# Output projection of a hybrid decoder block: where its weight buffers lie, in which order its transfers are queued, and how its norm sums are made

## Chip, cores and metric

The kernel is one program on one NeuronCore of a Trainium2 chip. The metric is the device time of one execution in microseconds (us). Engine names are those of the profile: PE is TensorE's matmul row, PEld its weight loads, DVE VectorE, ACT ScalarE, POOL GpSimd, SP SyncE. SP, ACT and POOL also issue transfers (DMAs).

## The reference

One block for 512 tokens of width 2048, in float32, with one batch and one layer:

```python
h = _rmsnorm(x, norm1_g) * (1.0 + sc1) + sh1
p = h @ w_in                                    # 2048 x 4384
y_rwkv = _rwkv7_mixer(p[..., :N_RWKV_COLS], ...)  # 16 heads of 64, delta-rule state
y_pool = _pool_mixer(p[..., N_RWKV_COLS:], ...)   # causal means over 2, 4, 8, 16 tokens
mix = jnp.concatenate([y_rwkv, y_pool], axis=-1) @ w_out   # 2048 x 2048
x = x + gt1 * mix
h = _rmsnorm(x, norm2_g) * (1.0 + sc2) + sh2
x = x + gt2 * _conv_ffn(h, w_up, conv_w, conv_b, w_down)   # 2048 x 11264, 5632 x 2048
return _rmsnorm(x, norm_f_g)
```

The shifts, scales and gates (sh, sc, gt) come from `silu(c) @ w_ada + b_ada`. `_rmsnorm` needs, for each token, the sum of squares over all 2048 features.

## The kernel before, in words

**Layout.** Features lie on the 128 partitions, tokens on the free axis, so x is 16 tiles of 128x512. Every float32 operand of the large products is split in two F32R parts, a high part (a cast by ACT) and a low part (the rest, by DVE), and a product is three matmuls: high by high, high by low, low by high (`mm3`, lines 136 to 138). A matmul's stationary operand is a 128x128 piece of a weight tile, its moving operand an activation tile of 256 or 512 columns.

**Stages.** First the modulation rows and the first product tiles. Then the mixer, with the input projection interleaved (`projection`, line 646: 27 tiles of 48 matmuls, 512 columns wide) in an order that a planner writes out by hand. Then the output projection, the subject here. Then the up projection with the conv, then the down projection. From the output projection on, the work is a list of steps which `pipeline` (line 1257) emits: for step i its matmuls, then the load of step i + 4 (LA = 4), the split of step i + 2, then the `after` functions of step i.

**The output projection** has four kinds of steps:

- Early blocks (`out_block`, 7 of them, 12 matmuls 512 wide) still run beside the mixer's end.
- `late_blocks`: 9 steps of 12 matmuls, 512 wide. Their after functions also make sums and differences of activation halves (`operands0`), which the next group needs.
- `out_group`: 4 rounds of 7 steps p1 to p7, each of 24 matmuls 256 wide, which is a Strassen-like scheme for half of the rows and columns. Steps p3 and p6 need a *sum* of two weight blocks. It is made by a plain load into a `wide` tile (line 1488, SP) and a second load by POOL that adds to it (line 1489, `accum_op=ALU.add`). Steps p1, p2 and p7 end in `stage_pair` (line 1432): ACT scales the result into a staging tile and POOL adds it into x by an accumulating DMA (line 1437). From round 1 on, p2 and p4 also call `out_done` (line 1527), which squares a finished x tile for the norm and stores it (line 1529, POOL).
- `out_halves`: 16 steps for the first token half (`lo`), 16 for the second (`hi`), 12 matmuls 256 wide each. Each `lo` step loads 256 KB of weights four steps before its matmuls.

After them `first_steps` begins the up projection (24 matmuls 256 wide a step).

**Weight buffers.** A split weight lies in one of two places. `wp` tiles `whi` and `wlo` (four of each) come from the pool at the right end of the memory; `wtile` (names `ow`, later `uw`) are three-part tiles in pool `ea`, whose parts are used from byte offset 64 (`off=16` floats) or 0. In the program as laid out, `whi` and `wlo` begin at byte addresses that are 0 mod 128, and a `wtile` begins at 0 mod 128, so its parts with `off=16` are at 64 mod 128. The moving operands are at 0 mod 128. The up and down projections use `wtile`s at offset 64 for 256 columns and at 0 for 512. In the output projection the ring of `split2` goes `wtile`, `wtile`, `wp`, `wp`; the late blocks and most halves are in `wp`.

**Order of issue.** Within an engine's queue the framework's scheduler orders instructions by its own estimate of when they are ready, unless `tc.issue_after` pins one behind another.

**Norm.** `norm_rows` sums the squares over partitions with four 1-column matmuls (line 185), takes ACT's Sqrt (line 190), a reciprocal on DVE (191), scales an identity by it (194), and `norm_bcast` spreads it with a float32 matmul (line 198). This is done for each token half, in `out_halves` and in `first_steps`, and again at the kernel's end.

Of the kernel before, what the change touches and what calls it, by code (L numbers as in the profile page):

```python
# [9 lines left out]
F32 = mybir.dt.float32  # L10
F32R = mybir.dt.float32r
# [57 lines left out]
def block_kernel(ctx, tc, a, out, stop=None, dbg=None):  # L69
# [50 lines left out]
    def load_weights(src, eng=nc.sync):  # L120
        raw = wp.tile([P, WC], F32, tag="wraw", name="wraw", bufs=4)
        eng.dma_start(raw, src)
        return raw
# [1097 lines left out]
    def wide(name):  # L1221

        return rb.tile([P, 4, HT], F32, tag="wide", name=name, bufs=3)
# [8 lines left out]
    def x2(f, sl=slice(0, T)):  # L1232
        return x2q[f // 4][:, f % 4, sl]
# [15 lines left out]
    nsplit, lo_of, hi_of, g_of = [0], [None], [None], [None]  # L1249

    class Step:

# [42 lines left out]
    def residual(f, pss, gate, acc, lo, hi, fresh):  # L1295
# [48 lines left out]
    for t, i0 in ((mixa, 4), (mixb, 8)):  # L1344
        for i in range(4):
            nc.sync.dma_start(t[:, i, :], mixd[MIX_ORDER[i0 + i]])
    x2q += [None] * 4

    def load_x2(q):
        x2q[q] = quad(q, "x2")  # L1350
        nc.sync.dma_start(x2q[q], a["xT"][:, 4 * q : 4 * q + 4, :])

# [5 lines left out]
    M += last_mix  # L1358
    for q in range(3):
        load_x2(q)  # L1360

    ngate = ea.tile([P, 3 * NF], F32, tag="ncw", name="ngate")
    V.tensor_scalar(ngate[:, 0:KT], mod[:, 32 : 32 + KT], -1.0, None, op0=ALU.mult)

# [21 lines left out]

    def osplit(raw, w=None, i=0):
        if w is None:
            hi, lo = (wp.tile([P, WC], F32R, tag=t, name=t, bufs=4) for t in ("whi", "wlo"))
        else:  # L1390
            hi, lo = (w[:, 16 + o + i * WC : 16 + o + i * WC + WC] for o in (0, 2 * QW))
        hi_of[0] = S.copy(hi, raw)
        lo_of[0] = V.tensor_tensor(lo, raw, hi.bitcast(F32), op=ALU.subtract)
        return hi, lo
# [3 lines left out]

    nring = [0]

    def split2(src):
        i = nring[0] % 4
        nring[0] += 1
        if i > 1:
            return [osplit(src[:, j * WC : j * WC + WC]) for j in range(2)]
        w = wtile(i)
        hi, lo = w[:, 16 : 16 + 2 * WC], w[:, 2 * QW + 16 : 2 * QW + 16 + 2 * WC]
        hi_of[0] = S.copy(hi, src)
        lo_of[0] = V.tensor_tensor(lo, src, hi.bitcast(F32), op=ALU.subtract)
        return [(hi[:, j * WC : j * WC + WC], lo[:, j * WC : j * WC + WC]) for j in range(2)]  # L1410
# [17 lines left out]
    def add_pair(f, hs, ps, sign=1):  # L1428
        for j in range(2):
            add_x2(f + j, hs, ps[:, j * HT : (j + 1) * HT], sign)  # L1430

    def stage_pair(f, hs, ps, sign=1):
        t = wp.tile([P, WC], F32, tag="wraw", name="stage", bufs=4)
        for j in range(2):
            g = mod[:, 32 + f + j : 33 + f + j] if sign > 0 else ngate[:, f + j : f + j + 1]
            S.activation(t[:, j * HT : (j + 1) * HT], ps[:, j * HT : (j + 1) * HT], AF.Copy, scale=g)
        G.dma_start(x2q[f // 4][:, f % 4 : f % 4 + 2, hs], t[:, :].rearrange("p (f t) -> p f t", f=2), accum_op=ALU.add)

    def raw_step(f, k0, mm, after, **kw):
        d = {}  # L1440

        def load():
            d["w"] = load_weights(a["wout"][f, :, k0 * P : k0 * P + WC])

        return Step(None, mm, after, load, split=kw.pop("split", None) or (lambda: osplit(d["w"])), **kw), d

    def late_blocks():
        out_, prep = [], operands0()
        for f, k0 in [(f, 12) for f in (4, 5, 6, 7, 0, 1, 2)] + [(3, 0), (3, 12)]:
            def mm(wh, wl, f=f, k0=k0):  # L1450
                if k0 == 0:
                    pss[f] = bank()
                block(pss[f], wh, wl, k0, slice(0, T), k0 == 0, k0 > 0, (f, k0) == (3, 12))
            done = [lambda f=f: add_x2(f, slice(0, T), pss[f])] if k0 else []
            out_.append(raw_step(f, k0, mm, [lambda: next(prep, None)] + done, hold=(f, k0) == (3, 12))[0])
        return out_

    o4 = []

    def out_group():  # L1460
# [8 lines left out]
        def buf(i):  # L1469
            while len(o4) <= i // 2:  # L1470
                o4.append(ea.tile([P, 4 * QW], F32, tag=f"t4{len(o4)}", name="ow4"))
            return o4[i // 2][:, (W1, W2)[i % 2]]

# [5 lines left out]
        for h in range(4):  # L1479
            f, d = 2 * h, {}  # L1480

            def plain(i, r, g):
                return lambda: nc.sync.dma_start(two(buf(i)), src(r, g))

            def both_(name, r1, g1, r2, g2, d=d):
                def load():
                    d[name] = wide(name).rearrange("p a b -> p (a b)")
                    nc.sync.dma_start(two(d[name]), src(r1, g1))
                    G.dma_start(two(d[name]), src(r2, g2), accum_op=ALU.add)
                return load  # L1490
# [32 lines left out]
        for h in range(4):  # L1523
            seq += out_[h][:5] + firsts[h + 1 : h + 2] + out_[h][5:]
        return seq

    def out_done(f):
        sumsq(acc, x2(f), 0, T, f == 0, o4[1][:, 2 * QW + f % 2 * T : 2 * QW + f % 2 * T + T])
        G.dma_start(x2d[f], x2(f))

    def half_done(f, hs, ps):
        add_x2(f, hs, ps)
        sumsq(acc, x2(f, hs), hs.start, hs.stop, False)
        G.dma_start(x2d[f][:, hs], x2(f, hs))

    first = {}

    def out_halves():
        kept, raws = {}, {}
# [12 lines left out]

        def raw(f, e):
            raws[f, e] = load_weights(a["wout"][f, :, 12 * e * P : 12 * e * P + WC])
# [19 lines left out]
        for j, (f, e) in enumerate(again):  # L1574
            hi[j].split = lambda f=f, e=e: kept[f, e]
        for j, n in zip((0, 1, 2, 3, 6, 7, 8, 9), range(8)):
            hi[j].load = lambda n=n: raw(*order[n])
        for j, i in ((1, 0), (3, 1)):
            hi[j].after[:0] = [lambda i=i, e=e: in_ea(8 + i, e, i) for e in range(2)]
        for n in range(4, 8):  # L1580
            hi[n + 1].after[:0] = [lambda n=n: in_wp(*order[n])]
        steps = first_half()
        hi[1].after.append(lambda: first.update(dg=norm_rows(acc[:, H0])))
        hi[3].after.append(lambda: first.update(rstd=norm_bcast(first["dg"])))
        for j in (4, 5, 6, 7, 9, 10, 11, 12):
            hi[j].after.append(lambda: next(steps, None))
# [86 lines left out]
    def first_steps():  # L1673
# [3 lines left out]
        for n in range(NB):  # L1677
            d = {}

            def load(sl, n=n):  # L1680
                if not rows:
                    rows.extend(ea.tile([P, 4 * QW], F32, tag=f"t4{i}", name="wrow") for i in range(2))
                nc.sync.dma_start(rows[n % 2][:, sl], a["wup"][2 * n, :, sl])

# [27 lines left out]
    halves, ups = out_halves(), first_steps()  # L1712
# [4 lines left out]
    pipeline(late_blocks() + out_group() + halves + ups)  # L1717
    for _ in steps:
# [208 lines left out]
    yd = [tc.dram_tile([P, T], F32, name=f"yd{f}") for f in range(KT)]  # L1927

    def queue(*args, **kw):
        with tc.issue_after(g_of[0].ins) if g_of[0] else nullcontext():  # L1930
            g_of[0] = G.dma_start(*args, **kw)

# [373 lines left out]
```

## Time and profile before

| | us |
|---|---|
| median of 3 runs | 2169.04 |
| lowest and highest of them | 2135.17, 2174.9 |
| profiled execution, its own time | 2138.61 |
| its span, first to last instruction | 2136.6 |

| engine | busy us | share of the span |
|---|---|---|
| PE | 2097.3 | 98% |
| PEld | 1874.0 | 88% |
| DVE | 1703.0 | 80% |
| ACT | 1055.4 | 49% |
| POOL | 262.0 | 12% |

A matmul's row in the profile gives the time from its start to its modelled end. Matmuls are pipelined, so that is longer than the distance from one start to the next; the distance is had from a stretch of the timeline divided by the matmuls in it.

### The profile page before, as it was taken

How to read it: one execution, taken by the hardware profiler on the slowest of the kernel's cores; microseconds unless marked ns; L12 is line 12 of the kernel's file. 1: busy time of each engine (PE TensorE's matmuls, PEld its weight loads, DVE VectorE, ACT ScalarE, POOL GpSimd, SP SyncE). 2: the span in 40 equal slices, each digit the busy share in tenths (PEclk: the TensorE clock that was granted, in tenths of full speed). 3: DMA queues.
4: the chain of work that ended last, by engine and by line, in shares of the span. 5: the costliest groups of instructions: out<-in, count | busy, mean ns of one | idle time of the engine just before them, and what ended most of it. 6: DMA issues, size and time to landing. Idle time of an engine off the chain costs nothing.

```text
span 2136.6 us, 44762 instructions
## 1 busy us (share of the span) xinstructions
PE 2097.3 (98%) x18216; PEld 1874.0 (88%) x18216; DVE 1703.0 (80%) x2649; ACT 1055.4 (49%) x1520; POOL 262.0 (12%) x400
## 2 busy tenths in 40 slices
PE   7999999999989999999999999999999999999997
PEld 3567777777767999999999999999999889998897
DVE  7988898989857867988888888877878658767775
ACT  4354444434434547655555555555556544453353
POOL 0002122211210321110011001000000000021100
PEclk9999999999999999999999999999999999999999
DMA  9966666656537975988988888877777645488865
GB/s 394 406 227 198 199 195 178 191 174 177 166 106 253 246 216 166 323 246 250 257 252 242 248 260 248 227 211 209 207 206 215 217 143 138 135 268 319 313 209 177
DMA packets 175792, 481.37 MB, mean 225 GB/s; under 512 B 21521, under 2 KB 32737, under 8 KB 166753
## 3 DMA queue, kind: packets, MB, share of 16 engines
q1 hardware_dynamic: 120914, 353.17, 47.9%
q0 software_dynamic: 33456, 87.59, 20.1%
q10 hardware_dynamic: 21216, 37.76, 5.8%
q8 instruction: 143, 2.34, 0.4%
q14 instruction: 63, 0.52, 0.1%
HBM read 438.05 MB, written 37.23 MB: 222 GB/s over the span
## 4 chain that ended last, share of the span: by engine, by line
PE 86%; issue 5%; DMA 3%; DVE 3%; ACT 1%; POOL 1%; POOLq 0%; DVEq 0%; ACTq 0%
PE b L138 21%; PE b L136 21%; PE b L137 21%; PE mm L646 10%; PE pf L427 4%; PE pb L1048 1%; DVE war L765 1%; PE pa L712 1%; DMA wa<-ada 1%; DMA wraw<-win 0%; PE pf L136 0%; PE pf L138 0%; PE pf L137 0%; POOL x L888 0%; PE pb L1088 0%
## 5 line engine op out<-in xcount | busy, mean ns | idle before, releaser
L138 PE MATMUL b<-t,uw 128*128 128x256 f32 x1408 | 388.6, 276 | 0.0
L136 PE MATMUL b<-t,uw 128*128 128x256 f32 x1408 | 388.6, 276 | 0.0
L137 PE MATMUL b<-t,uw 128*128 128x256 f32 x1408 | 388.6, 276 | 0.0
L136 PE MATMUL b<-y,uw 128*128 128x256 f32 x1056 | 292.0, 277 | 0.0
L137 PE MATMUL b<-y,uw 128*128 128x256 f32 x1056 | 291.6, 276 | 0.0
L646 PE MATMUL mm<-ahl,whi 128*128 128x512 f32 x864 | 289.6, 409 | 2.1 <-DVE rk L549 1.4
L138 PE MATMUL b<-y,uw 128*128 128x256 f32 x1056 | 291.5, 276 | 0.0
L138 PEld LDWEIGHTS b<-t,uw 128*128 128x128 f32 x1408 | 264.3, 188 | 0.0
L137 PEld LDWEIGHTS b<-t,uw 128*128 128x128 f32 x1408 | 264.3, 188 | 0.0
L136 PEld LDWEIGHTS b<-t,uw 128*128 128x128 f32 x1408 | 264.2, 188 | 0.0
L1619 DVE TENSOR_TENSOR uw<-r,uw 128x1024 fp32r<-128x1024 f32 x164 | 200.6, 1223 | 79.0 <-ACT uw L1618 78.7
L1619 DVE TENSOR_TENSOR uw<-wquart,uw 128x1024 fp32r<-128x1024 f32 x148 | 181.1, 1223 | 54.6 <-ACT uw L1618 54.5
L1618 ACT CAST uw<-r 128x1024 fp32r<-128x1024 f32 x164 | 172.8, 1053 | 73.0 <-PE b L138 73.0
L1619 DVE TENSOR_TENSOR uw<-wd,uw 128x1024 fp32r<-128x1024 f32 (+1 forms) x112 | 124.2, 1109 | 100.5 <-ACT uw L1618 100.5
L136 PE MATMUL b<-act,uw 128*128 128x256 f32 (+1 forms) x608 | 200.6, 330 | 0.0
L137 PE MATMUL b<-act,uw 128*128 128x256 f32 (+1 forms) x608 | 200.4, 330 | 0.0
L138 PE MATMUL b<-act,uw 128*128 128x256 f32 (+1 forms) x608 | 200.3, 330 | 0.0
L136 PEld LDWEIGHTS b<-y,uw 128*128 128x128 f32 x1056 | 198.3, 188 | 0.1
L137 PEld LDWEIGHTS b<-y,uw 128*128 128x128 f32 x1056 | 198.2, 188 | 0.0
L138 PEld LDWEIGHTS b<-y,uw 128*128 128x128 f32 x1056 | 198.1, 188 | 0.0
L646 PEld LDWEIGHTS mm<-ahl,whi 128*128 128x128 f32 x864 | 158.2, 188 | 43.2 <-issue 12.2
L1618 ACT CAST uw<-wquart 128x1024 fp32r<-128x1024 f32 x148 | 155.8, 1053 | 80.7 <-PE b L138 65.5
(406 smaller groups left out, 4812.4 us busy)
## 6 DMA issues: line engine op xcount, KB each, us to landing
wquart<-wup SPq DMA_DIRECT2D x176, 512.0 KB, 6.0
wa<-ada SPq DMA_DIRECT2D x48, 1024.0 KB, 9.5
war<-ada SPq DMA_DIRECT2D x192, 256.0 KB, 3.8
wd<-wdn SPq DMA_DIRECT2D x64, 512.0 KB, 4.6
wraw<-win ACTq DMA_DIRECT2D x118, 256.0 KB, 4.1
wquart<-wup POOLq DMA_DIRECT2D x44, 512.0 KB, 6.7
r<-wup SPq DMA_DIRECT2D x44, 512.0 KB, 4.6
r<-wup POOLq DMA_DIRECT2D x44, 512.0 KB, 8.1
```

The source lines that it names most:

```text
L136: muls = [lambda: PE.matmul(ps, wh, xh, start=start, stop=False, skip_group_check=more), lambda: PE.matmul(ps, wh, xl, start=False, stop=F ...
L137: lambda: PE.matmul(ps, wh, xl, start=False, stop=False, skip_group_check=more),
L138: lambda: PE.matmul(ps, wl, xh, start=False, stop=stop, skip_group_check=more)]
L427: PE.matmul(pf[n % 2 * 4 + ii], w[:, sl], full[k], start=k == 0, stop=k == KT - 1)
L646: PE.matmul(ps, w[:, sl], x, start=first, stop=k == KT - 1 and i == 2)
L712: PE.matmul(ps, pw[:, i, d * P : (d + 1) * P], zs[i], start=i == 0, stop=i == 1)
L765: V.scalar_tensor_tensor(wa, wa, 1.0, cqs[kq], op0=ALU.mult, op1=ALU.mult, accum_out=modq[:, kq, j : j + 1])
L1048: PE.matmul(pt[HS[e], h, c * 2 * L : (c + 1) * 2 * L], nt[HS[e], s, :], rw[HS[e], s, :, :], start=True, stop=True)
L1618: hi_of[0] = S.copy(hi, src)
L1619: lo_of[0] = V.tensor_tensor(lo, src, hi.bitcast(F32), op=ALU.subtract)
```

## The change

- 64 bytes of padding (`edge`) are put at the front of the `tables` and of the `wts` pool. `whi` and `wlo` move by 64 bytes to 64 mod 128; activations stay at 0 mod 128. This holds for all stages that use `wp`, the mixer's input projection too.
- The late blocks (512 wide) are split into `wtile`s at offset 0. The ring of `split2` begins with `wp`.
- All of POOL's transfers in the group and the halves go through `queue`, and SP's through `loadq`: each is pinned behind the one emitted before it. Splits are pinned in the same way (`parts`).
- The plain load of a p3 or p6 sum is issued one step earlier (`begin`); the accumulating load stays four steps ahead.
- The staging tile of `stage_pair` leaves the ring of four `wraw` tiles and uses two halves of a `t41` buffer. `out_done` squares into a PSUM bank in place of a buffer.
- Halves load their weights eight steps ahead, into four `wraw` tiles and four pieces of `t40`.
- x tiles are loaded in another order and partly later.
- The two norms of this stage use `norm_parts` and `norm_sum`: the sum of squares is split in two F32R parts, two 256-wide matmuls with a matrix of ones add over partitions and spread at once, and ACT's Ln and Exp make the inverse root. The norm at the kernel's end is unchanged.

```diff
+    tp.tile([P, 16], F32, tag="edge", name="edge")
+    wp.tile([P, 16], F32, tag="edge", name="edge", bufs=1)
...
+    def queue(*args, **kw):
+        with tc.issue_after(g_of[0].ins) if g_of[0] else nullcontext():
+            g_of[0] = G.dma_start(*args, **kw)
+
+    def loadq(*args):
+        with tc.issue_after(p_of[0].ins) if p_of[0] else nullcontext():
+            p_of[0] = nc.sync.dma_start(*args)
...
+    def norm_parts(acc):
+        t = rb.tile([P, 4, HT], F32R, tag="wide", name="sums", bufs=3)
+        S.copy(t[:, 0, :], acc)
+        V.tensor_tensor(t[:, 1, :], acc, t[:, 0, :].bitcast(F32), op=ALU.subtract)
+        return t
+
+    def norm_sum(t):
+        psb = bank()[:, 0:HT]
+        for i in range(2):
+            PE.matmul(psb, onesr, t[:, i, :], start=i == 0, stop=i == 1)
+        S.activation(psb, psb, AF.Ln, bias=eps[:, 0:1], scale=1.0 / D)
+        S.activation(psb, psb, AF.Exp, scale=-0.5)
+        return psb
...
-    for q in range(3):
+    for q in (1, 0):
         load_x2(q)
...
+    def parts(hi, lo, raw):
+        with tc.issue_after(hi_of[0].ins) if hi_of[0] else nullcontext():
+            hi_of[0] = S.copy(hi, raw)
+        with tc.issue_after(lo_of[0].ins) if lo_of[0] else nullcontext():
+            lo_of[0] = V.tensor_tensor(lo, raw, hi.bitcast(F32), op=ALU.subtract)
...
-    nring = [0]
+    nring = [2]
...
     def stage_pair(f, hs, ps, sign=1):
-        t = wp.tile([P, WC], F32, tag="wraw", name="stage", bufs=4)
+        t = buf(3)[:, nstage[0] % 2 * WC : nstage[0] % 2 * WC + WC]
+        nstage[0] += 1
...
-        G.dma_start(x2q[f // 4][...], ..., accum_op=ALU.add)
+        queue(x2q[f // 4][...], ..., accum_op=ALU.add)
...
+        def late_split(i, raw):
+            if i % 2 == 0:
+                w[i] = wtile(i // 2 % 2)
+            return osplit(raw, w[i - i % 2], i % 2, 0)
...
+        out_[2].after.append(lambda: load_x2(2))
...
             def both_(name, r1, g1, r2, g2, d=d):
                 def load():
+                    queue(two(d[name]), src(r2, g2), accum_op=ALU.add)
+
+                def begin():
                     d[name] = wide(name).rearrange("p a b -> p (a b)")
-                    nc.sync.dma_start(two(d[name]), src(r1, g1))
-                    G.dma_start(two(d[name]), src(r2, g2), accum_op=ALU.add)
+                    loadq(two(d[name]), src(r1, g1))
+                load.begin = begin
                 return load
...
+        for st, nxt in zip([begun] + seq, seq):
+            if nxt.load and hasattr(nxt.load, "begin"):
+                st.load = lambda a=nxt.load.begin, b=st.load: (a(), b() if b else None)
...
     def out_done(f):
-        sumsq(acc, x2(f), 0, T, f == 0, o4[1][:, 2 * QW + f % 2 * T : 2 * QW + f % 2 * T + T])
-        G.dma_start(x2d[f], x2(f))
+        sumsq(acc, x2(f), 0, T, f == 0, bank() if f else None)
+        queue(x2d[f], x2(f))
...
+        def raw(f, e, slot=0):
+            if slot > 3:
+                raws[f, e] = o4[0][:, (slot - 4) * WC : (slot - 3) * WC]
...
         for b, (f, e) in enumerate(order):
-            lo[b].load = lambda f=f, e=e: raw(f, e)
+            early = lambda f=f, e=e, b=b: raw(f, e, b % 8)
+            if b < 4:
+                then = group[b - 4].load
+                group[b - 4].load = lambda early=early, then=then: (then() if then else None, early())
+            else:
+                lo[b - 4].load = early
...
+        hi[1].after.insert(0, lambda: first.update(t=norm_parts(acc[:, H0])))
+        hi[2].after.append(lambda: first.update(rstd=norm_sum(first["t"])))
...
-        out_[1].after.append(lambda: norm1.update(dg=norm_rows(acc[:, H1])))
-        out_[3].after.append(lambda: norm1.update(rstd=norm_bcast(norm1["dg"])))
+        out_[1].after.append(lambda: norm1.update(t=norm_parts(acc[:, H1])))
+        out_[2].after.append(lambda: norm1.update(rstd=norm_sum(norm1["t"])))
```

More of the change, by code (lines that the diff above doesn't have):

```diff
@@ L1358, in block_kernel @@
     M += last_mix
-    for q in range(3):
+    for q in (1, 0):
         load_x2(q)
-    ngate = ea.tile([P, 3 * NF], F32, tag="ncw", name="ngate")
-    V.tensor_scalar(ngate[:, 0:KT], mod[:, 32 : 32 + KT], -1.0, None, op0=ALU.mult)
+    ngate = drv[:, 0:KT]
+    onesr = ea.tile([P, 3 * NF], F32R, tag="ncw", name="onesr")[:, 0:P]
+    S.copy(onesr, ones)
+    V.tensor_scalar(ngate, mod[:, 32 : 32 + KT], -1.0, None, op0=ALU.mult)
     TO = {}
@@ L1454, in late_blocks, with out_group @@
             done = [lambda f=f: add_x2(f, slice(0, T), pss[f])] if k0 else []
-            out_.append(raw_step(f, k0, mm, [lambda: next(prep, None)] + done, hold=(f, k0) == (3, 12))[0])
-        return out_
-    o4 = []
-    def out_group():
+            st, d = raw_step(f, k0, mm, [lambda: next(prep, None)] + done, hold=(f, k0) == (3, 12))
+            st.split = lambda i=len(out_), d=d: late_split(i, d["w"])
+            out_.append(st)
+        out_[2].after.append(lambda: load_x2(2))
+        return out_
+    def out_group(begun):
         out_, firsts = [], []
@@ L1533, in half_done, with out_halves @@
         sumsq(acc, x2(f, hs), hs.start, hs.stop, False)
-        G.dma_start(x2d[f][:, hs], x2(f, hs))
+        queue(x2d[f][:, hs], x2(f, hs))
     first = {}
-    def out_halves():
+    def out_halves(group):
         kept, raws = {}, {}
@@ L1551, in steps_of @@
             return out_
-        def raw(f, e):
-            raws[f, e] = load_weights(a["wout"][f, :, 12 * e * P : 12 * e * P + WC])
+        def raw(f, e, slot=0):
+            if slot > 3:
+                raws[f, e] = o4[0][:, (slot - 4) * WC : (slot - 3) * WC]
+                loadq(raws[f, e], a["wout"][f, :, 12 * e * P : 12 * e * P + WC])
+            else:
+                raws[f, e] = wp.tile([P, WC], F32, tag="wraw", name="wraw", bufs=4)
+                loadq(raws[f, e], a["wout"][f, :, 12 * e * P : 12 * e * P + WC])
         def in_ea(f, e, i):
@@ L1575, in out_halves @@
             hi[j].split = lambda f=f, e=e: kept[f, e]
[L1576 to L1579, printed above, removed]
-        for n in range(4, 8):
[L1581 to L1585, printed above, removed]
+        for j, n in zip((-2, -1, 0, 1, 8, 9, 10, 11), range(8)):
+            (lo + hi)[16 + j].load = lambda n=n: raw(*order[n])
+        hi[1].after.insert(0, lambda: first.update(t=norm_parts(acc[:, H0])))
+        hi[2].after.append(lambda: first.update(rstd=norm_sum(first["t"])))
+        for j, i in ((2, 0), (3, 1)):
+            hi[j].after += [lambda i=i, e=e: in_ea(8 + i, e, i) for e in range(2)]
+        steps = first_half()
+        for n in range(4, 8):
+            hi[n + 3].after[:0] = [lambda n=n: in_wp(*order[n])]
+        for j in (3, 4, 5, 6, 8, 9, 10, 11):
             hi[j].after.append(lambda: next(steps, None))
@@ L1682, in load @@
                     rows.extend(ea.tile([P, 4 * QW], F32, tag=f"t4{i}", name="wrow") for i in range(2))
[L1683 removed]
+                loadq(rows[n % 2][:, sl], a["wup"][2 * n, :, sl])
             def mul(d, key, Y):
@@ L1716, in block_kernel @@
         ups[i].load = None
-    pipeline(late_blocks() + out_group() + halves + ups)
+    pipeline(late_ + group + halves + ups)
     for _ in steps:
```

41 lines of the change are left out of this document (21 added, 20 removed).

## The prediction

> **What bounds the kernel now.** I read the engine shares first, then PE's waits around the output projection, then its timeline in stretches.
>
> ```profile
> PE 2097.3 (98%) x18216; PEld 1874.0 (88%) x18216; DVE 1703.0 (80%) x2649; ACT 1055.4 (49%) x1520; POOL 262.0 (12%) x400
> PE b L198 <- DVE rdiag L194: 1.8, 1, 1.8
> PE b L136 <- ACT whi L1392: 1.1, 1, 1.1
> PE b L138 <- DVE wlo L1393: 0.2, 1, 0.2
> 691.30:836.10 144.80, 141.65 (x1168) 0.99 0.78 206
> 836.10:2120.80 1284.70, 1284.46 (x10460) 1.00 0.78 231
> ```
>
> The last three waits are all that PE has between 691 and 836 us (who waits, for whom, us in total, times, longest). The two stretches give length, PE's busy time with its matmuls, granted clock, DMA share and GB/s. PE is busy all through the up and down projections, and the change ends at about 836 us: there the pools at the right end are closed and addresses are as before. So only the distance from one matmul to the next, and PE's few stalls, can move the time.
>
> ```profile
> 692.35:697.46 5.11, 5.11 (x47) 1.00 1.10 243
> 697.46:703.21 5.75, 5.75 (x50) 1.00 0.95 261
> 703.21:708.87 5.66, 5.66 (x51) 1.00 0.80 248
> 703.21:765.93 62.72, 62.72 (x530) 1.00 0.98 236
> 839.04:898.88 59.84, 59.84 (x530) 1.00 0.85 298
> ```
>
> Each row counts two or three matmuls that are in flight at its edges. The last two hold 22 steps, 528 matmuls 256 wide each, with no wait in either: 118.8 ns a matmul in the group, 113.3 in the up projection. The second row, two steps with weights in `whi` and `wlo` at 0 mod 128, gives 5.75 / 48 = 119.8. The third, two steps with weights in `wtile`s at 64 mod 128, gives 117.9. Yet the first, also `wtile`s at 64 but just behind the late blocks, gives 5.11 / 45 = 113.6. So 64 mod 128 is not enough: after a stretch at 119.8, PE keeps a slower step until something breaks it.
>
> Against 113.3 the stretch from 691.3 to 836.1 has 1152 matmuls of 256 columns (28 x 24 + 32 x 12 + 4 x 24), 130.5 us, and three of 512, 0.7. Of its 144.8 us, 13.6 are above that floor. No more can come from here.
>
> **The change part by part.** *Width and address.* 576 matmuls (14 group steps and 20 halves) have weights in `whi` or `wlo` here: 576 x (119.8 - 113.3) = 3.7 us. The 528 others that lie behind them (432 in the group and the halves, 96 in the first up steps) go from 117.9 to 113.3: 2.4. Together 6.1 us, all on PE's path. I take the whole, since the new order enters the group as the first row above did.
>
> The Trainium skill (SBUF — State Buffer, "SBUF: two separate sides") says that PE, ACT and DVE's dedicated ports never wait on anyone, and TensorE: Matmul & The Clock Gate ("Back-to-back issue gap") gives N / 2.4 + 2.5 ns, an estimate of 109 ns for 256 columns, with no term for the weights' address. By them these 6.1 us would be nothing. The trace disagrees: 119.8 and 113.3 at one width, one data type and full clock.
>
> The same padding moves `whi` and `wlo` under matmuls 512 wide, which now lie at 0.
>
> ```profile
> 667.22:680.82 13.60, 13.60 (x62) 1.00 0.97 360
> L646 PE MATMUL mm<-ahl,whi 128*128 128x512 f32 x864 | 289.6, 409 | 2.1 <-DVE rk L549 1.4 <-DVE v L549 0.7
> L646 PE MATMUL mm<-ahl,wlo 128*128 128x512 f32 x432 | 174.4, 404 | 0.2 <-DVE wlo L622 0.2
> by line: PE mm L646 42.6%; issue 3.8%; PE pb L1048 2.8%; DVE war L765 2.4%; DMA wraw<-win 1.9%; PE pa L712 1.8%; POOL x L888 1.6%; PE pb L1088 1.6%; PE py L1113 1.5%; PE py L1118 1.5%; DMA dx<-xyl 1.4%; PE pa L955 1.3%; PE pb L917 1.3%; PE
> ```
>
> In the first row 60 matmuls of the out blocks take 226.7 ns each at 0 mod 128, twice 113.3, so that is their floor too. At 64 no row shows them. If 512 columns mind the wrong half as 256 do, each costs 6.5 ns more, and 1296 in the mixer (the L646 rows), 120 in the first tiles and 84 in the early blocks make 9.8 us; if not, nothing. A gain below 226.7 I exclude, as no long row is under it. The mixer isn't all PE's: in the chain of waits from 150 to 645 us (last row), L646 has 42.6% of 495 us, 211 us, or about 930 matmuls at their floor. So 0 to 9.8, on the path 0 to 930 x 6.5 + 1.3 = 7.3. I take 3, nearer to nothing, since the 512-wide rows have shown no slow step so far. The nine late blocks keep 0 mod 128 and cost nothing.
>
> *Loads of the halves.*
>
> ```profile
> 780.36:785.06 4.70, 3.38 (x26) 1.00 0.95 324
> 778.93 3.35 DMA wraw<-wout
> 774.37 6.34 SPq L122 DMA_DIRECT2D wraw<-wout  x5
> L1436 ACT ACTIVATE stage<-b,mod x16: 462/468/476, 696.3 to 761.3; 128x256 f32<-128x256 f32 x16
> L1437 POOL DMA_DIRECT2D x<-stage x12: 1183/1227/1741, 698.4 to 774.7; - x12
> ```
>
> Two halves with 24 matmuls take 4.70 us where 2.88 (at 119.8) are due: the wait for ACT above. The chain there (second row: start, us) goes back to a load of `wraw` at 778.93, and SP's queue shows five such loads spread over 6.34 us, since the staging tiles share the ring. With eight pieces, loaded eight steps (10.9 us) ahead, the load is hidden: 1.8 us gone. What is late next is the cast by ACT, 0.6 us in each step of 1.36, so it stays covered. A load behind another waiting one in SP's fixed order would bring back at most the same 1.8.
>
> *Norm.*
>
> ```profile
> 799.51:809.67 10.16, 8.33 (x56) 0.83 0.46 131
> 829.62:839.04 9.42, 9.42 (x80) 1.00 0.70 214
> 801.19 1.28 ACT L190 ACT_TABLE_LOAD   x1
> 802.49 0.26 ACT L190 ACTIVATE rstd<-b,eps 128x2 f32<-128x2 f32 x1
> 797.52 0.42 ACT L1290 ACTIVATE sqx<-x 128x256 f32<-128x256 f32 x1 [0.95 <-DVE x L1426]
> ```
>
> The first norm's stretch has 48 matmuls of the halves: 10.16 us against 24 x 0.1179 + 24 x 0.1198 = 5.7, so 4.5 for the norm. PE waited 1.8 us for the scaled identity, behind a 1.28 us table load and 0.26 us of Sqrt, and then ran at a mean clock of 0.83. The second stretch has 72: 9.42 against 8.5, 0.9. The new form needs two matmuls of 0.113 each time, 0.5 in all; ACT's Ln and Exp come after them, 0.42 each by the 256-wide row, and PE doesn't need the result before the up projection. Split and sum ahead of the matmuls are two operations of some 0.42, put a step later than the old sums were. So 5.4 - 0.5 = 4.9 us go; at worst one step's wait, 1.4 us, comes back. Should Ln need a table load, 1.28 us fall on ACT, half idle there.
>
> *POOL's order.* Here the change adds a wait.
>
> ```profile
> L1489 POOL DMA_DIRECT2D r<-wout x8: 1183/1200/1707, 682.7 to 746.6; - x8
> DMA to landing us min/median/max: 6.9/9.0/11.9
> 686.29 2.43 POOL L1489 DMA_DIRECT2D r<-wout  x2 [2.35 <-PE pb L137]
> 698.36 1.19 POOL L1437 DMA_DIRECT2D x<-stage  x1 [9.63 <-issue]
> L1408 ACT CAST ow<-r x8: 1042/1048/1052, 690.5 to 756.6; 128x1024 fp32r<-128x1024 f32 x8
> L1409 DVE TENSOR_TENSOR ow<-r,ow x8: 1216/1226/1226, 691.6 to 758.4; 128x1024 fp32r<-128x1024 f32 x8
> ```
>
> Now three accumulating loads (L1489) go ahead of the first staging transfer at 698.36, which waits for PE. That is why no sum is late. In emission order, the sum for step i + 4 stands behind the staging transfer of step i - 1. Counted from the start of step i of 2.72 us: two ACT scalings 0.94, the staging issue 1.23, then the accumulating load, which lands 6.9 to 11.9 us (median 9.0) after its start: at 9.1 to 14.1. It must be split (1.05 + 1.22) before step i + 4 starts at 10.9, so it must land by 8.6. Four p6 sums are so placed, each late by 0.5 to 5.5, 2.6 at the median; the three later p3 sums stand behind a store that waits for nothing new and have about 1.5 us more room. Behind a late sum wait its casts, and behind these, on ACT, the next scalings. Sum: 4 x 0.5 = 2 us at the quick landing, 4 x 2.6 + 3 x 1.1 = 13.7 at the median, 34 if every landing is the slowest. That one is of loads issued together (x2 at 686.29), which the fixed order spreads out, so I leave it out; the others I put between quick and median: 6. For the range I keep 0 (if half of a split tile lets PE begin) to 13.7.
>
> *The rest.* Fewer x loads ahead of the late blocks let go a wait of 0.3 us at 681. Squares go to a PSUM bank, one of eight; ACT and DVE do as much as before.
>
> The sum on the profiled execution: -6.1 - 1.8 - 4.9 - 0.3 + 6 + 3 = -4.1. From its 2138.6 us that gives 2134.5. The three runs shown lie from 2135 to 2175 around 2169, 30 above the profiled execution, and no row tells what the longer ones have more. The forecast stands on the footing of the profile; the upper end of the range takes that spread.
>
> **The rivals.**
>
> *All gains, no costs.* Landings near 7 us, 512 columns indifferent: -13.1, 2125.5. For it: no wait for any sum now. Against it: the fixed order.
>
> *Slower by the fixed order and the moved weights.* Place: p6 of each round, and the mixer. Price: 13.7 + 7.3 - 13.1 = +8, 2146.5. It decides at landings over some 9 us, or a 512-wide distance above 226.7 by more than 3 ns.
>
> *A slow step that stays.* The new norm has no float32 matmul to shake PE. What lies behind it:
>
> ```profile
> L136 PE MATMUL b<-act,uw 128*128 128x512 f32 x288 | 112.1, 389 | 0.0
> ```
>
> Of the 10,460 matmuls from 836 to 2121 us, three times these 288 are 512 wide; the other 9,600, entered at 117.9, cost 4.6 ns more each, up to +44: 2178. For it: slow steps held from 703 to 836 us here, ending at the second norm. Against: the new stage should never enter one.
>
> *The width part does nothing*: 119.8 and 113.3 have another cause than the address, so gains of 7.0, no cost in the mixer, 6 at POOL: -1, 2137.6. It is what the two pages of the Trainium skill above would have. Against it: the rows at 113.3 and 119.8.
>
> **How the numbers follow.** Forecast (2127 to 2140) 0.50; all gains 0.14; slower by order and weights 0.24; slow step 0.05; width does nothing 0.07. The likeliest case's own range is 2127 to 2140. For all: 2120 below, and 2172 above, which takes in the slower rival and the spread of runs. 2% is 43 us, about what a measurement of this kernel can tell from no change; only the slow step reaches it, for slower. For faster nothing in the trace does, since the floor allows 13.6; what I leave there is for the spread of the runs. So faster 0.07, same 0.88, slower 0.05.
>
> **What would show it.** Right: 113.3 ns a matmul from 691 us through the halves; no wait for `rdiag` or for `whi` at 780; waits of PE for casts of `r`, one to three us each, at p6 steps; L185 and L198 left at the kernel's end alone; L646's stretches a little longer. Wrong: group steps of 2.83 us or more, no waits at p6, or a mixer that ends 7 us later.

## The result, and the profile after

The kernel after is slower: 2189.8 us, median of six runs (2185.33 to 2194.47), against 2156.43 for before over six runs beside it. Against the three quicker ones of these (median 2140.4) the ratio is 1.0232, interval 1.0203 to 1.026. The forecast of 2134.5 and its range (2120 to 2172) missed.

Runs of most of these kernels fall into two groups some 33 us apart; in all fourteen profiled executions the group goes with the matmul distance that the up projection keeps (113.3 or 117.8 ns, below), and the other runs are sorted by their time alone, so kernels are compared here by their runs of the quicker group, called comparable. For before these are 17 of the 66 runs made beside all the kernels here, with the median 2138.6, which is also its profiled execution. By their times all six of after are of that kind, so 51 us are to be found: in the profiled executions, 2194.47 less 2138.6, 56.

The engine shares of after, then PE's waits from 640 to 900 us, then PE in stretches:

```profile
PE 2120.9 (97%) x18208; PEld 1891.4 (86%) x18208; DVE 1703.1 (78%) x2645; ACT 1052.5 (48%) x1524; POOL 261.3 (12%) x400
PE b L138 <- DVE x L1459: 27.5, 6, 7.4
PE mm L138 <- ACT ow L1418: 6.0, 1, 6.0
PE b L138 <- ACT whi L1418: 4.4, 1, 4.4
PE b L140 <- DVE uw L1679: 2.8, 1, 2.8
663.56:672.48 8.92, 2.97 (x13) 0.77 1.00 389
672.48:681.00 8.52, 8.52 (x25) 0.64 0.64 211
711.78:824.00 112.22, 80.30 (x564) 0.83 0.66 153
711.78:721.00 9.22, 3.02 (x27) 0.93 0.44 111
721.00:726.23 5.23, 5.23 (x25) 0.50 1.03 144
870.50:877.71 7.21, 4.40 (x27) 0.76 0.35 109
900.00:959.84 59.84, 59.84 (x530) 1.00 0.93 317
```

In before, PE's waits between 691 and 836 us were 3.1 us. Here are three new places.

*The start of the late blocks.* PE waits 6.0 us for a cast of the first block's weights, then runs at a granted clock of 0.64: 24 matmuls of 512 take 8.5 us where 5.6 were due. Some 9 us in all.

*The group of half-width products.* From 711.78 to 824 us, 562 matmuls are worth 66.2 us at 117.8 ns, and take 112.2. PE idles for 31.9 of the 46 extra (112.22 less 80.30), in seven waits: 23.0 before the four p6 steps and 9.0 before three p7 steps, each two steps further on. The other 14.1 are lost to matmuls at half clock. The fourth and fifth of these rows show one pair: a step with 6.2 us of idle time, then a step at a clock of 0.50, 24 matmuls in 5.2 us.

*The start of the up projection.* One wait of 2.8 us for the first `uw`, and slow matmuls behind it: 7.2 us for 24 matmuls that take 2.7.

9 + 46 + 4.5 is 60; the gains further down take some of it back. The last row is the up projection at 113.3 ns, the same as before.

The late start is SP's order. SP's queue, first of before, then of after (start, length, number of transfers):

```profile
650.24 4.07 SPq L122 DMA_DIRECT2D wraw<-wout  x4
657.41 2.98 SPq L1346 DMA_DIRECT2D mixa<-mixd  x4
```

```profile
656.28 3.27 SPq L1261 DMA_DIRECT2D mixa<-mixd  x4
659.60 1.85 SPq L1261 DMA_DIRECT2D mixb<-mixd  x4
661.50 0.91 SPq L1261 DMA_DIRECT2D x<-xT  x2
662.50 12.41 SPq L1261 DMA_DIRECT2D wraw<-wout  x7
```

Before, the first four weights of the late blocks are asked for at 650 us, ahead of the mixer's outputs. In emission order they come behind ten other transfers, at 662.5, and PE wants them at 666.

The group's waits are POOL's order. POOL's and ACT's instructions around the first of them, and three of the longest waits between 640 and 900 us:

```profile
704.70 1.21 POOL L1255 DMA_DIRECT2D x<-ow  x1 [14.78 <-ACT ow L1477]
705.44 1.68 POOL L1255 DMA_DIRECT2D r<-wout  x1
719.04 1.19 POOL L1255 DMA_DIRECT2D x<-ow  x1 [11.92 <-ACT ow L1418]
719.77 1.68 POOL L1255 DMA_DIRECT2D r<-wout  x1
715.97 1.14 ACT L1418 CAST whi<-r 128x512 fp32r<-128x512 f32 x2 [8.31 <-DMA r<-wout]
717.01 0.83 ACT L1477 ACTIVATE ow<-b,mod 128x256 f32<-128x256 f32 x2
727.26 1.14 ACT L1418 CAST whi<-r 128x512 fp32r<-128x512 f32 x2 [7.54 <-DMA r<-wout]
POOL x L1255 <- ACT ow L1477: 94.6, 10, 14.8
ACT ow L1418 <- DMA r<-wout: 35.4, 4, 11.5
ACT whi L1418 <- DMA r<-wout: 25.5, 3, 9.6
```

Read it as a chain. The accumulating load of a sum (`r<-wout`, issued at 705.44) lands just ahead of the cast at 715.97, where the bracket shows ACT idle for 8.31 us for it. ACT casts, and only then scales the staged pair (717.01). POOL, which waits for that pair, issues the staging transfer at 719.04 and behind it the next accumulating load at 719.77; its cast starts at 727.26, and ACT has again waited 7.54. Each late sum makes the next one late. POOL waits 94.6 us for the scalings in this way, and ACT 60.9 for sums. In before the same two waits, from 660 to 840 us, are 16.5 and 4.5:

```profile
POOL x L1437 <- ACT stage L1436: 16.5, 4, 6.5
ACT ow L1408 <- DMA r<-wout: 4.5, 1, 4.5
```

For six of the seven waits PE's own row names L1459, DVE's add of a finished product into x. DVE's and PE's instructions at the first wait:

```profile
716.62 1.29 DVE L1420 TENSOR_TENSOR wlo<-r,whi 128x512 fp32r<-128x512 f32 x2 [8.15 <-ACT whi L1418]
719.95 0.87 DVE L1459 SCALAR_TENSOR_TENSOR x<-b,mod,x 128x256 f32<-128x256 f32 x2
720.97 0.55 PE L138 MATMUL b<-y,whi 128*128 128x256 f32 x1 [6.20 <-DVE x L1459]
```

Step p6 adds onto the PSUM bank that holds p4's product, so the add that reads this product must come first, and it stands in DVE's order behind the low part of the late sum. The low part is ready at 717.91, the add at 720.82, and PE starts at 720.97: the last 3.1 of its 6.2 us are for the add. The p7 steps wait in the same way for p6's add, which stands behind the low part of the next round's p3 sum.

### The profile page after: what moved, and what is told of

Same layout as the page of the kernel before. It is cut to its first block, busy times and chain, and to the rows that moved or that the text cites. A ratio compares the mean times of both kernels' runs of the same rounds, so it can differ in the third digit from the quotient of the medians.

```text
span 2192.4 us, 44738 instructions
## 1 busy us (share of the span) xinstructions
PE 2120.9 (97%) x18208; PEld 1891.4 (86%) x18208; DVE 1703.1 (78%) x2645; ACT 1052.5 (48%) x1524; POOL 261.3 (12%) x400
## 4 chain that ended last, share of the span: by engine, by line
PE 79%; issue 9%; DMA 5%; DVE 4%; ACT 2%; POOL 1%; POOLq 0%; SPq 0%; DVEq 0%; ACTq 0%
PE b L138 19%; PE b L140 19%; PE b L139 19%; PE mm L648 10%; PE pf L429 4%; DMA r<-wout 1%; DVE war L767 1%; DMA wraw<-wout 1%; PE pb L1050 1%; DMA wa<-ada 1%; PE pa L714 0%; DMA war<-ada 0%; DVE wlo L624 0%; PE pf L140 0%; PE pf L138 0%
```

## The experiments

**One order at a time.** Between them the first three give up POOL's order through the output projection, SP's, and both.

```diff
     def queue(*args, **kw):
-        with tc.issue_after(g_of[0].ins) if g_of[0] else nullcontext():
-            g_of[0] = G.dma_start(*args, **kw)
+        G.dma_start(*args, **kw)
     def loadq(*args):
-        with tc.issue_after(p_of[0].ins) if p_of[0] else nullcontext():
-            p_of[0] = nc.sync.dma_start(*args)
+        nc.sync.dma_start(*args)
```

POOL's alone:

> The changed kernel with POOL's transfers of the output projection no longer pinned in emission order; all else stays. Theory A (POOL's fixed order puts each accumulating load behind a staging transfer that itself waits for the casts of the sum before, a loop of some 11 us a sum): the group's seven waits, about 34 us, and the half-clock matmuls behind them, about 14 us, go; the wait at the first late block (6 us) stays: 2190 becomes about 2145. Rival B (two staging halves instead of four tiles, or the DMA engines' load, make the sums late): less than 10 us comes back, 2180 or more.

SP's alone:

> The changed kernel with SP's loads no longer pinned; POOL stays pinned. Theory A: the 6 us wait and its slow clock at the first late block go (their weights are no longer queued behind the loads of the mixer's results), about 9 us, and the sums stay late, since they wait for POOL and not for their plain loads: about 2181. Rival C (the plain loads come too late in SP's fixed order): the group's waits go too, 2145 or less.

Both:

> Both queues free, splits still pinned, with the new addresses, norm and deeper loads. Theory A: all three waits of the group's kind go, and what the change gains is left: 113 to 118 ns a matmul, no wait of the halves' loads, shorter norm: 2125 to 2137, under the kernel before's quick runs by 0 to 12 us. If B or C holds in part, it stays above 2150.

PE's waits without POOL's order, the group's longest without SP's, then those without both, and there twelve steps of the group:

```profile
PE mm L138 <- ACT ow L1417: 5.7, 1, 5.7
PE b L138 <- DVE x L1458: 5.4, 3, 4.3
PE b L140 <- DVE uw L1678: 2.8, 1, 2.8
```

```profile
PE b L138 <- DVE x L1458: 31.9, 6, 6.4
```

```profile
PE b L138 <- DVE x L1457: 2.0, 1, 2.0
PE b L140 <- DVE uw L1677: 1.1, 1, 1.1
698.15:732.07 33.92, 33.92 (x290) 1.00 1.07 276
```

Without POOL's order the group's waits fall from 32 to 5.4 us, the late start stays, and the comparable runs have the median 2155.0 (2158.86 over all ten), 35 less than after and 10 above the 2145 expected. Without SP's order the late start is gone, the group's waits stay, and the four comparable runs have 2182.6 (2183.13 over all six), 7 less. Without both it is 2138.93 over all ten runs, and 2137.4 over the eight comparable ones (2134.75 to 2142.14). So the two orders make the whole 51 us, POOL's most of it. They don't simply add: giving up SP's order saves 7 us beside POOL's order and 17 without it (2155.0 less 2137.4), where the waits left, 13.9 us in the first of these views, fall to 3.1.

The profiled execution without POOL's order is one at the other distance:

```profile
900.00:959.84 59.84, 59.84 (x510) 1.00 0.91 266
```

Over the same 59.84 us it has 510 matmuls where after has 530, which makes 117.8 and 113.3 ns. This holds from 850 to some 1715 us. It took 2187.97 us, 33 more than the kernel's comparable runs.

**The addresses alone.** The kernel before with the two edge tiles and the late blocks' weights in `wtile`s:

```diff
+    tp.tile([P, 16], F32, tag="edge", name="edge")
+    wp.tile([P, 16], F32, tag="edge", name="edge", bufs=1)
...
-    nring = [0]
+    nring = [2]
...
+            st.split = lambda i=len(out_), d=d: late_split(i, d["w"])
```

> The kernel before with the padding, the late blocks in three-part tiles at offset 0 and the ring begun with the other buffers; queues, loads and norm as before. By the price of the prediction: 6 us less in the group and halves, if they run at 113.3 ns; 0 to 7 us more in the mixer, whose 512-wide matmuls now go at 233.3 ns: 2132 to 2146 beside 2139 for an undisturbed run of the kernel before. If a slow step of 118 ns is entered after the late blocks and kept, 3 us less only in the group and up to 44 more behind it: to 2180.

```profile
PE b L138 <- DVE x L1428: 5.3, 1, 5.3
PE b L138 <- ACT ow L1394: 4.9, 1, 4.9
```

Median 2183.53 of four (2156.46 to 2186.64); the ratio to before, 1.0101 with the interval 0.9981 to 1.0221, has both groups of runs in it. Three of the four are of the other group; the profiled one, among them, kept 117.8 through the up projection. Group by group the kernel takes 17 us more than before beside it (2156.46 against 2138.8, 2186.25 against 2169.5), above both forecasts. There are two waits that before hasn't, 10.2 us together and with half clock behind them, and no gain shows: the group runs at 117.8 ns. What makes the two waits wasn't followed up. By itself this part of the change is a loss; without both orders, above, the same addresses show neither wait, so this loss doesn't explain after.

**The first loads alone.** After, with four loads outside SP's order:

```diff
-            loadq(d["w"], a["wout"][f, :, k0 * P : k0 * P + WC])
+            (nc.sync.dma_start if k0 == 12 and 3 < f < 8 else loadq)(d["w"], a["wout"][f, :, k0 * P : k0 * P + WC])
```

> The kernel after, with the loads of the first four late blocks' weights taken out of SP's fixed order; all else as after. Theory (the late start is a cost of its own, made by SP's order): PE's wait of 6.35 us at the late blocks and the half-clock matmuls behind it, 2.6 us more, are gone, the group's seven waits (34 us) stay within 4 us of that sum, and the time is 2177 to 2184. Rival (the two orders share one cost, so that what is saved at the start comes back in the group): the group's waits grow by 6 us or more and the time stays at 2187 to 2194.

```profile
663.56:673.00 9.44, 9.44 (x43) 1.00 1.01 367
```

The wait is gone at full clock. The group's waits are the same seven, and the median is 2184.86 (1.022 of before's comparable runs beside it), 5 us less than after, just over the 2177 to 2184 expected. The late start is a cost of its own, and the smaller one.

**The link on ACT, first try.** The scalings of a staged pair are freed of their place behind the casts:

```diff
-            with tc.issue_after(hi_of[0].ins), tc.issue_after(lo_of[0].ins):
-                for fn in todo:
-                    fn()
+            for fn in todo:
+                if getattr(fn, "free", False):
+                    fn()
...
```

> The kernel after, with ACT's scalings of the staged sums no longer ordered behind the casts of the step after next; POOL's and SP's fixed orders stay. Theory (a loop: late sum, casts on ACT, staging behind the casts, staging transfer, next sum on POOL, landing; taking out the link on ACT opens it): the group's waits fall from 34 us to under 12, the time by 25 to 40 us, to 2150 to 2165. Rival (POOL's order alone makes each sum late, ACT's place is no part of it): waits of 25 us or more stay and the time is 2180 to 2194.

```profile
PE b L138 <- DVE x L1462: 28.3, 6, 7.1
```

The comparable runs took 2188.1 and 2188.8 (median of all four 2205.81), the waits are those of after. But ACT's instructions came out in the very order of after: freed, they were put in the same place. The run decides nothing on the loop; it is a second measurement of after.

**The sums in an order of their own.** On POOL the accumulating loads follow one another, staging transfers and stores follow one another, and nothing ties the two:

```diff
+    def sumq(*args, **kw):
+        with tc.issue_after(l_of[0].ins) if l_of[0] else nullcontext():
+            l_of[0] = G.dma_start(*args, **kw)
...
-                    queue(two(d[name]), src(r2, g2), accum_op=ALU.add)
+                    sumq(two(d[name]), src(r2, g2), accum_op=ALU.add)
```

> The kernel after, with the accumulating loads of the sums ordered among themselves only, and the staging transfers and stores in a fixed order of their own; SP's order, both halves of the staging tile and ACT's order stay. Theory (the sum standing behind the staging transfer is what makes it late): the group's waits fall from 34 us to under 10, the wait at the late blocks stays at some 6 us, and the time is 2150 to 2165, as with POOL's order given up altogether (2158.9). Rival (two staging halves instead of four, or where the sums' tiles come free, make it late): waits of 20 us or more stay, 2175 to 2194.

```profile
PE b L138 <- DVE x L1465: 5.7, 1, 5.7
PE mm L138 <- ACT ow L1424: 5.3, 1, 5.3
```

Median 2154.19 over all ten runs, 2150.9 over the seven comparable ones; one of the group's waits is left, and the late start. The two staging halves were as in after, and ACT's scalings still stood behind the casts (later in the group even one pair of casts further back), so it was the sum standing behind the staging transfer.

**Without the edges.** Both orders given up, and the two edge tiles removed:

```diff
-    tp.tile([P, 16], F32, tag="edge", name="edge")
-    wp.tile([P, 16], F32, tag="edge", name="edge", bufs=1)
```

> The kernel after with POOL's and SP's orders given up (as in the run at 2138.9 us) and without the two edge tiles, so that the two weight rings lie at 0 mod 128 as in the kernel before; the late blocks' pairs of tiles and the deeper loads stay. Theory (the edges bring little either way: the mixer isn't PE's, and the group keeps a slow distance anyway): the mixer ends within 2 us of where it ends with the edges although its long rows go back from 233.3 to 226.7 ns; the group's steps from these rings take 119.8 ns a matmul instead of 117.8, some 2 us; total within 4 us of 2139. Rival (my prediction's term: 233.3 ns costs the mixer up to 7.3 us on the path): the mixer ends 5 to 7 us earlier and the time is 2132 to 2135. If the distance of 117.8 ns is kept through the up projection, 34 us come on top, whatever the edges do.

Where the out block on `pb` begins says how long the mixer took. In one profiled execution each, in the ten kernels with the edges it begins at 643.1 to 647.3 us, 645.3 in the mean; in the four without, at 641.0 to 645.2, 643.6 in the mean. The difference is 1.7 us, with single executions 2 us to either side, so a cost of the wrong half to the mixer isn't clear of the spread, and the rival's 5 to 7 us aren't seen. The nine comparable runs of this kernel have the median 2133.3, 4 under the kernel with its edges (3 when each is taken against before's runs beside it; ratio to before 0.9984, interval 0.9956 to 1.0012). That time is the rival's, 2132 to 2135, and not the theory's, but it doesn't come from the mixer as the rival had it. The edges cost a little, if anything, and bring nothing that can be seen.

**The link on ACT, second try.** ACT's scalings of a staged pair are now put ahead of the next casts:

```diff
             ahead(i + LA, load)
+            for fn in st.stage:
+                fn()
             ahead(i + 2, split)
...
-            S.activation(t[:, j * HT : (j + 1) * HT], ps[:, j * HT : (j + 1) * HT], AF.Copy, scale=g)
+            with tc.issue_after(hi_of[0].ins):
+                hi_of[0] = S.activation(t[:, j * HT : (j + 1) * HT], ps[:, j * HT : (j + 1) * HT], AF.Copy, scale=g)
```

> The kernel after, with ACT's scalings of a staged sum put ahead of the casts of the step after next instead of behind them; POOL's and SP's fixed orders stay. The run before this one that meant to open this link left ACT's order as it was; this one changes it. Theory (a loop makes each late sum cause the next: its casts hold back ACT's scalings, these the staging transfer, this the next sum): without the link only the fixed distance is left, 2 to 4 us late for some four to six sums, so the group's waits fall from 34 us to 10 to 18 and the time to 2162 to 2176, less some 5 us if the casts now come late themselves. Rival (no loop; POOL's fixed distance alone makes the waits): 28 us or more of waits stay and the time is 2182 to 2195.

```profile
PE b L138 <- DVE x L1463: 10.7, 4, 7.3
PE b L138 <- ACT whi L1422: 5.0, 2, 3.8
```

Median 2169.87, 20 less than after, with POOL's and SP's orders unchanged. The group's waits are 15.7 us instead of 32. So about half of them came from the loop, though the sums also landed later here (median 10.2 us, 8.6 in after). Of the rest, the run with the sums' own order keeps 5.7; by that subtraction some 10 us go with the fixed distance on POOL.

**Both mends together.** The sums' own order and the four free loads:

> The kernel after with the two mends tried one by one together: the sums' accumulating loads in an order of their own on POOL, and the first four late blocks' loads outside SP's order; all else as after. Theory (the two costs are separate and add): no wait at the late blocks (5.5 us and 1.5 of half clock less than in the run with the sums' order alone), the group keeps one wait of some 6 us, the start of the up projection its 3, and the time is 2140 to 2147, or 34 us more in runs that keep the distance of 117.8 ns through the up projection. Rival (an earlier start only makes the sums later by as much): group waits of 12 us or more, 2149 to 2156.

```profile
PE b L138 <- DVE x L1465: 4.2, 1, 4.2
PE b L140 <- DVE uw L1685: 2.8, 1, 2.8
```

Median 2142.54. The ratio to before, 0.9883 with the interval 0.9851 to 0.9915, tells nothing of the change, since twenty of before's twenty-one runs there were of the other group. The seven comparable runs have 2142.4, 8.5 us less than with the sums' order alone, where the loads by themselves gave 5: the two gains add. 47 of the 51 us are taken back with all other orders left in place, and 4 are still missing to before.

**The parts that gain.** First what is left when orders, edges and the late blocks' `wtile`s are undone, in effect before with the new norm and the deeper loads (the splits stay pinned, the staging tiles stay moved):

> The kernel after without its pinned orders, without the edge tiles, and with the late blocks' weights back in the two rings: in effect the kernel before with the new norm, the deeper loads and the moved staging tiles. Theory (norm and loads are the two parts that gain, 4.9 and 1.8 us by the prediction): 5 to 7 us under the kernel before where both run the up projection at 113.3 ns, 2130 to 2134. Rival (the start of the up projection, now reached before its inputs are ready, gives back 2 to 4 us): 2134 to 2138.

```profile
PE b L136 <- ACT whi L1414: 4.5, 1, 4.5
```

Six runs at 2135.13 to 2144.88, median 2136.38: the rival's range, not the theory's 2130 to 2134, though the wait that the rival named is only 0.3 us in the profile. The longest is the profiled one, with a wait of 4.5 us in the group that was not followed up. Then the norm alone:

```diff
-        hi[1].after.append(lambda: first.update(dg=norm_rows(acc[:, H0])))
-        hi[3].after.append(lambda: first.update(rstd=norm_bcast(first["dg"])))
+        hi[1].after.append(lambda: first.update(t=norm_parts(acc[:, H0])))
+        hi[2].after.append(lambda: first.update(rstd=norm_sum(first["t"])))
```

> The kernel before with the new norm sums alone. Theory (prediction's step: the wait for the scaled identity and the slow clock behind it go, two short matmuls come): the stretch of the first norm falls from 10.16 us to 6 or less, the second from 9.42 to some 9, no wait at either; 4 to 5 us under before in runs at the same distance in the up projection, 2133 to 2136. Rival (ACT's logarithm and exponential with their table loads hold back the casts or the inputs of the up projection): PE waits 1.3 us or more there and the gain is under 3 us.

```profile
PE b L136 <- ACT whi L1409: 1.1, 1, 1.1
798.86:805.07 6.21, 6.17 (x53) 1.00 0.44 133
827.73:836.50 8.77, 8.68 (x77) 1.00 0.79 257
```

The first norm's stretch, again with 48 matmuls of the halves, takes 6.21 us instead of 10.16, the second 8.77 instead of 9.42: 4.6 together. The longest wait left is the one at the halves that before has too. Comparable runs 2132.46 to 2136.92, median 2134.4, 4.2 under before, close to the 4.6 of the two stretches. By these medians the new norm alone beats both kernels, before by 0.2% (ratio to that job's before 0.9855, interval 0.9809 to 0.9902, which has the two groups mixed in it); the deeper loads add nothing that shows above the spread.

## Why the prediction was wrong

**POOL's order: the step that failed.** That the p6 sums come late behind the staging transfers was right, and so was the arithmetic of the first lateness; the size was not. I took 6 us from 0 to 13.7, and the group lost 46: 31.9 idle and 14.1 to half clock. Three terms were missing.

- *The loop.* I counted each sum from the start of a step that was on time, and wrote that the next scalings wait behind the late casts, but gave that no price. Opened, it gives back some 20 us; the 15.7 us of waits that then remain are close to my upper end.
- *The path to PE.* I let PE wait for a split weight alone, at the steps of the late sums. It waits for DVE's adds too, which stand behind the late sum's low part: 3.1 us of the first p6 wait, and the three waits at p7 steps, 9.0 us, where I had put none.
- *The clock.* I priced a wait at its own length. Here each wait of 3.8 us or more is followed by matmuls of 213 ns (427 at 512 columns), 14.1 us in the group and 2.9 at the late blocks. The prediction had the same sign before it, in the norm's stretch at a clock of 0.83, and used it only there. The Trainium skill (TensorE: Matmul & The Clock Gate, "Part 1: The HAM clock gate (the "warmup" mystery)") says that PE falls to half clock after an idle window of about 3.4 us and returns after as much busy time. The trace agrees: 0.50 over the 5.23 us from 721 us, behind 6.2 idle. It also shows it behind shorter waits than that, so here the measurement decides: behind the group's two waits of 2.6 us, which come soon after a longer one, and behind the single wait of 2.8 us at the start of the up projection. The 2.0 us in the run without both orders brought none.

The landings were not the fault. In after, the sums on POOL take

```profile
DMA to landing us min/median/max: 6.3/8.6/12.1
```

which is the row that I quoted, or a little better. I named 34 us as the sum "if every landing is the slowest" and left it out; that PE's waits came to 32 is near it by chance only.

**SP's order: a step that was missing.** I weighed it for the halves alone, at most 1.8 us. I looked at the x loads that leave the queue and not at the late blocks' weights that fall behind ten transfers. It cost 9 us in the profiled execution. Letting the first four loads go gave back 5 to 8.5, giving up SP's whole order 7 beside POOL's and 17 without it.

**The start of the up projection** I didn't price either: 2.8 us and slow matmuls behind it. The fast halves reach it before ACT and DVE have normed and split its inputs; the wait is there without both orders too (1.1 us).

**Width and address: the reason was half right, the gain too small to see.** The rows that I read hold here: 256-wide matmuls with weights at 0 mod 128 take 119.8 ns, and no long row of them less; 512-wide ones at 64 take 233.3, in every one of their long rows:

```profile
643.12:648.72 5.60, 5.60 (x25) 1.00 0.41 132
851.12:856.90 5.78, 5.78 (x52) 1.00 0.51 145
```

The first row is 24 matmuls in 5.60 us in after, where before took 5.44. But the right half only allows the short distance. The group kept 117.8 ns with every weight at 64, with both orders or with neither, so most of the 6.1 us didn't come: 119.8 became 117.8, some 0.7 us for its 336 matmuls from `whi` and `wlo`, and only part of the halves took 113.3. That it "enters the group as the first row did" was the choice that failed. The mixer's price, 3 in my sum and up to 7.3, came out at 1.7, within the spread; the late blocks, at 0 mod 128 but behind 512-wide rows at 64, took some 232 ns a matmul, 0.6 us in all. Of the rivals, "the width part does nothing" (0.07) described this part best.

**The slow step that stays** I gave 0.05. It shows in runs of most kernels here, by their times in none of after: 20 matmuls in 530 fewer over 60 us, 33 us in such a run. By their times 49 of before's 66 runs have it too; that would be the 30 us that I saw above the profiled execution and couldn't place. It made no part of the 51.

**Norm and halves: right.** The second row of the last view is after's first norm with 48 matmuls of the halves, 5.8 us without a wait (10.16 before); alone the norm gave 4.6 us of the 4.9 expected. At the halves no wait for `whi` is left, 1.1 us of PE's time; the 1.8 us that I priced for it don't show in the times.

The rival on the other side named one right place, the fixed order, and the wrong size: at +8 it was six times too small, and 7.3 of its price were for the mixer.

## What to carry to other kernels

When transfers are put in a fixed order, follow each one to what it waits for, and on to whether that waits, by way of another engine, for the transfer behind it: such a loop multiplies a small lateness by every round. Look for what else stands behind a late piece in each engine's order, here DVE's adds. Price PE's waits of some 3 us or more with the slow matmuls behind them, here nearly half as much again. A queue that gets a fixed order has a first element, too: look at what the old order had asked for long before the stage began.

## What the runs showed of the hardware

The distance between matmuls has a memory. With the same weights and addresses, 256-wide matmuls take 113.3 or 117.8 ns and keep that through 860 us of busy PE, over thousands of changes of weight and bank. With weights at 0 mod 128 they take 119.8; for 512 columns the good place is the other one, 226.7 at 0 and 233.3 at 64. Changes were seen behind waits with half clock (in after 24 matmuls take 2.74 us from 802.8 us, where 2.83 go with 117.8 ns), behind the two matmuls with ones (in after 117.8 ns up to them at 853 us, 113.3 behind), and in a few places where nothing stands out; what decides between the two isn't settled by these runs. It is worth some 33 us of this kernel, more than any gain of the change.
